# Two more experts' weight loads started in the transition, into memory of split operands and of the last blocks' sums

## The chip, the core and the metric

The kernel runs on one core of one Trainium2 chip. A core has five engines that each work through their own instructions in order: TensorE (PE in the profile; its weight loads are PEld), VectorE (DVE), ScalarE (ACT), GpSimd (POOL) and SyncE (SP, which here only issues transfers and reads registers). Sixteen DMA engines move data between the chip's memory (HBM) and the core's own memory (SBUF). The metric is the time of one execution on the device, in microseconds (us); the time given for the kernel before is the median of three runs.

## The reference

One decoder layer on a sequence of 1024 tokens with D_MODEL = 1024, all float32. Its second half is a hierarchical mixture of experts: 4 groups of 8 experts, each token takes the best group and in it the best two experts, so 2048 token-expert pairs go to 32 experts.

```
h = rms_norm(x) * (1 + sc1) + sh1                        # first half: a combined projection,
q, k, v, gu, gv, ga, gb = split(h @ w_in)                # windowed attention and a chunked gMLP,
x = x + g1 * (merged(q..gb) @ w_o)                       # merged by gates, then W_o
h = rms_norm(x) * (1 + sc2) + sh2
g_idx  = argmax(h @ w_router_g + b)                      # 1 of 4 groups
top_i  = top_k((h @ w_router_e + b)[g_idx], 2)           # 2 of its 8 experts
for each expert e, in blocks of at most 128 of its tokens xb:
    y = (silu(xb @ w_gate[e]) * (xb @ w_up[e])) @ w_down[e]   # 1024 -> 512 -> 1024
    out[tokens] += y * weight
x = x + g2 * out
return rms_norm(x, final_g)
```

The weights of one expert are three matrices of 2 MB each: gate, up and down.

## The kernel before

**Two stages.** The first, up to some 690 us, does the projections, the attention, the gMLP, W_o and the router. The second runs the 32 experts. Between them lies the transition: the router's results are counted and sorted, the tokens' rows h are stored to HBM (`h2d`), and the rows of the first experts are gathered from there.

**Order of the loads.** Every 2 MB matrix is an item of `ring2`, in the order gate0, up0, gate1, down0, up1, gate2, down1, up2, gate3, down2, up3, gate4, ...: item 7 is up2, item 8 gate3. An item goes into one of 7 buffers named `big`. `get(n)`, called where item n is used, first issues the loads up to item n+6; the SP queue issues them in order, and each waits until its buffer's last reader is through. Only the two halves of item 6 (down1) go through POOL's queue, around the first gather. Items 0 to 6 are issued before the transition ends; item 7 is the first that waits for a buffer that an expert has used.

**Units of work.** A unit is one expert or two. The first four experts stand alone, with blocks of 32, 32, 64 and 128 tokens (the units 0 to 3); after them come units of a block of 128 and one of 64 rows. A block under 128 rows multiplies float32 weights as they lie in the `big` buffer (`side`, L1504). For a block of 128 rows every matrix is split into a rounded part and the rest, in four pieces of 128x1024: ACT casts `hi` from `big` (L451) and DVE subtracts to get `lo` (L452), then 24 matmuls of three kinds follow (`mm3`, L135 to L137). There are three `hi` and three `lo` buffers, 512 KB each, in the pool `h2p`. gate3 (item 8) is the first matrix that is split; up2 (item 7) is used as it lies.

**What else stands on ACT and PE.** `x_t` transposes a block's gathered rows on PE (L1448, L1458); ACT copies the result out of PSUM as `xTh` (L1449, or L451 for a 128-row block). `a_t` does the same with the product sl of the silu (L1552, L1559 on PE; `aTh` on ACT, L1554 or L451). These copies stand on ACT in one row with the casts of the next weights. The order of the instructions on each engine is decided when the kernel is built, by a scheduler with its own idea of how long things take.

**The transition on POOL.** After the two halves of item 6 and the first two gathers, POOL issues the third gather (unit 2), works on the first two tables that list the experts' tokens (L1777, L1778; PE multiplies them at L1780), copies the gain vector into other layouts (`in_layout`, L1569, `g` from `g2r`, which PE spreads at L1826), issues the fourth gather (unit 3) and goes on with the tables. Earlier it clears the four accumulators z (L1657).

**The last blocks' sums.** For the last four experts the partial sums stay in the tiles `Z` and `YL` (2560 floats in a partition), used in the last units alone.

Of the kernel before, what the change touches and what calls it, by code (L numbers as in the profile page):

```python
# [10 lines left out]
F32 = mybir.dt.float32  # L11
F32R = mybir.dt.float32r
# [7 lines left out]
P = 128  # L20
D = 1024
# [5 lines left out]
FE = 512  # L27
# [9 lines left out]
FIRST = (0, 3, 2, 1)  # L37
# [17 lines left out]
class Ring:  # L55


    def __init__(self, bufs):
        self.bufs, self.items, self.tiles, self.issued = bufs, [], {}, 0

    def add(self, load):
        self.items.append(load)
        return len(self.items) - 1
# [4 lines left out]
            self.issued += 1  # L68

    def get(self, n):  # L70
        self.upto(n + self.bufs - 1)
        return self.tiles[n]


# [27 lines left out]
def block_kernel(ctx: ExitStack, tc: tile.TileContext, x, c, positions, rel_bias, w_ada, b_ada,  # L102
# [5 lines left out]
    w_gate, w_up, w_down = w_gate[0], w_up[0], w_down[0]  # L108
    PE, DVE, ACT, POOL, SP = nc.tensor, nc.vector, nc.scalar, nc.gpsimd, nc.sync

    def f(ap):
        return ap.bitcast(F32)
# [8 lines left out]
    def nm(s):  # L121
        uid[0] += 1
        return f"{s}_{uid[0]}"

    def bigt(shape, dt=F32):
        return big.tile([P] + shape, dt, name=nm("big"), tag="big")
# [333 lines left out]
    R = {}  # L460
# [860 lines left out]
    for i, js in ((4, w1), (5, w1), (6, w2), (7, w2)):  # L1321
        j = {4: 1, 5: 3, 6: 4, 7: 6}[i]
# [13 lines left out]
    ring2 = Ring(7)  # L1336
    jobs2 = Jobs(2)
# [19 lines left out]
    ends = flat[-4:]  # L1357
    regs = {}

    def expert_reg(c, eng):  # L1360
        if (c, eng) not in regs:
            regs[c, eng] = eng.value_load(ord_i[0:1, c:c + 1], min_val=0, max_val=NE - 1)
        return regs[c, eng]
# [5 lines left out]
    def parts_of(src):  # L1369

        return src.rearrange("(h p j) n -> p h (j n)", h=2, p=P)

    def w2_load(c, w, down, parts=1, eng=SP):
        def load():
            t = bigt([4, D] if down else [8, FE])
            th = t.rearrange("p (h j) n -> p h (j n)", h=2)
            if late:
                src = parts_of(w[8 * FIRST[c]])
                for i in range(2):
                    if late["stage"] == 0 and i == 1:  # L1380
                        gather(flat[0])
                    with tc.issue_after(R["gather" if late["stage"] or i else "h2d"].ins):
                        POOL.dma_start(th[:, i], src[:, i])
                if not late["stage"]:
                    gather(flat[1])
                late["stage"] += 1
                return t
            src = w[ds(expert_reg(c, eng), 1)].rearrange("a k n -> (a k) n") if c >= 4 else w[8 * FIRST[c]]
            src = parts_of(src)
            if parts == 1:  # L1390
                eng.dma_start(th, src)
            else:
                n = th.shape[2] * 2 // parts
                for h in range(2):
                    for k in range(0, th.shape[2], n):
                        eng.dma_start(th[:, h, k:k + n], src[:, h, k:k + n])
            return t
        return load
# [4 lines left out]
    def parts(i):  # L1403

        return P // rows_of.get(i, P)
# [19 lines left out]
    def gather(i, idx=None):  # L1425
        t = wk.tile([P, D], F32, name=nm("xg"), tag="xg")
        R["gather"] = fetch(t, h2d, IDX[i][0] if idx is None else idx, *x_rows(i))
        XG[i] = t

    Z, YL, adds = {}, {}, []  # L1430
# [134 lines left out]
    def in_layout(dst, src, q):  # L1565

        n, m = P // q, D // q
        for e in range(q):
            POOL.tensor_copy(dst[n * e:n * e + n], src[n * e:n * e + n, m * e:m * e + m])  # L1569
# [37 lines left out]
    i = 0  # L1607
# [26 lines left out]
    h2p = p2.enter_context(tc.tile_pool(name="p2hl", bufs=3, reuse_waits="tile"))  # L1634
    wk = p2.enter_context(tc.tile_pool(name="p2wk", bufs=2, reuse_waits="tile"))
# [15 lines left out]
    for i in range(2):  # L1651
        t = wk.tile([P, D], F32, name=nm("xg"), tag="xg")
        ACT.copy(t, zcol.to_broadcast([P, D]))
    for i in ends:
        Z[i] = wk.tile([P, D // parts(i)], F32, name=nm("z"), bufs=1)
        YL[i] = wk.tile([P, D // parts(i)], F32, name=nm("y"), bufs=1)
        POOL.memset(Z[i], 0.0)  # L1657
    fs = wk.tile([P, 12], F32, name="fs", bufs=1)

    ring2.upto(5)  # L1660
    late["stage"] = 0
    ring2.upto(6)
    late.clear()


    def combine_weights():
# [155 lines left out]
    def spread(dst):  # L1822

        for n in range(2):
            sl, ps = slice(512 * n, 512 * n + 512), bank()
            PE.matmul(ps, ones[0:1, :], dst[0:1, sl], start=True, stop=True)  # L1826
            ACT.copy(dst[:, sl], ps)
# [8 lines left out]
    nj = len(jobs2.jobs)  # L1836
# [49 lines left out]
    def l_put(j):  # L1886
        st_ = put(out, IDX[ends[j]][1], F["o"][j], parts(ends[j]))
        for other in F["puts"]:
            tc.declare_no_dep(st_.ins, other.ins, reason="a token's row is written once")
        F["puts"].append(st_)  # L1890

    def final():

        with tc.manual_schedule(engines={E_.DVE, E_.Activation, E_.Pool, E_.PE}):
# [27 lines left out]
            for j in (3, 0, 1, 2):  # L1922
                l_put(j)
    jobs2.hook(f_at, f_load)
    jobs2.hook(nj - 30, f_gain)
    jobs2.hook(nj - 20, lambda: (spread(F["g"]), in_layout(F[4], F["g"], 4), in_layout(F[2], F["g"], 2)))
    jobs2.hook(nj - 1, final)
# [4 lines left out]
    with tc.If(nover > 0):  # L1932
# [38 lines left out]
        with tc.For_i(0, nover, 1) as s:  # L1971
# [6 lines left out]
            for w, down in ((w_gate, False), (w_up, False), (w_down, True)):  # L1978
                t = bigt([4, D] if down else [8, FE])
# [7 lines left out]
            for z, key in ((0, "g"), (1, "u")):  # L1987
                PS[X, key] = bank()
                for kk in range(0, 8, 2):
                    wh, wl = split2(raws[z][:, kk:kk + 2])  # L1990
                    for q in range(2):
                        k = kk + q
# [14 lines left out]
        for t in range(8):  # L2007
            z, y = bigt([D]), bigt([D])
# [15 lines left out]
def build(inputs):  # L2024
    import concourse.bacc as _bacc

    nc = _bacc.Bacc("TRN2", target_bir_lowering=False, num_devices=1)
    arrays, args = {}, []
    for name in _INS:
        a = np.ascontiguousarray(inputs[name])  # L2030
        arrays[f"in_{name}_dram"] = a
        args.append(nc.dram_tensor(f"in_{name}_dram", a.shape, mybir.dt.from_np(a.dtype), kind="ExternalInput").ap())
    for i, (shape, dtype) in enumerate(_OUTS):
        dt = mybir.dt.from_np(np.dtype(dtype))
        args.append(nc.dram_tensor(f"out_{i}_dram", shape, dt, kind="ExternalOutput").ap())
    with tile.TileContext(nc) as tc:
        block_kernel(tc, *args)
    return nc, arrays
# [8 lines left out]
```

## Time and profile before

| | us |
|---|---|
| median of 3 runs (lowest, highest) | 1276.18 (1273.81, 1278.65) |
| profiled execution | 1273.97 |
| its span, first to last instruction | 1272.3 |
| PE busy in it | 1149.1 (90%) |
| DVE, ACT, POOL busy | 770.7, 554.9, 220.7 |
| mean granted TensorE clock | 0.951 of full speed |

The experts' stage takes the last 580 us or so of the span. A clock of 1.00 in a row is 2.4 GHz, 0.50 is 1.2 GHz. In rows of the timeline a bracket holds the idle time of the engine before the instruction and what ended it: "[1.62 <-ACT hi L451]" is 1.62 us of idling until ACT's instruction of line 451 had written `hi`.

### The profile page before, as it was taken

The numbers are of one execution on the slowest core, as the hardware profiler recorded it, in microseconds if no ns is written. First come the engines' busy times: TensorE is split into PE (matmuls) and PEld (weight loads), VectorE is DVE, ScalarE is ACT, GpSimd is POOL, SyncE is SP. The second block draws the span as 40 slices with busy tenths as digits, with TensorE's granted clock in tenths as the row PEclk, the third lists the DMA queues.
The fourth block names the chain that finished last, engine by engine and source line by source line (L and its number), as shares of the span: only waits on it lengthen the run. The fifth ranks groups of instructions, "written<-read, shape, count | busy, mean of one in ns | idle before, by whom it ended". The sixth has DMA issues, their size and how long they took to land. (4 is left out here: it accounts for less than half of the span.)

```text
span 1272.3 us, 18572 instructions
## 1 busy us (share of the span) xinstructions
PE 1149.1 (90%) x6873; PEld 878.3 (69%) x6874; DVE 770.7 (61%) x1685; ACT 554.9 (44%) x970; POOL 220.7 (17%) x325
## 2 busy tenths in 40 slices
PE   5999999999989999799996998998999998899961
PEld 3788887778878988688775665665665656676530
DVE  7668885567777888443498454664424635695115
ACT  4459743335525775233242344543414524674130
POOL 2600000111041000110034311121022121112201
PEclk9899999999989999899996999999999998999975
DMA  9734436547354445433956999999989999999994
GB/s 313 223 112 125 133 101 231 182 153 260 105 195 150 124 133 181 151 99 100 348 213 211 390 401 416 402 392 400 335 297 403 380 327 414 410 361 369 394 414 173
DMA packets 106345, 334.70 MB, mean 263 GB/s; under 512 B 7998, under 2 KB 52158, under 8 KB 81800
## 3 DMA queue, kind: packets, MB, share of 16 engines
q1 hardware_dynamic: 92438, 296.66, 61.4%
q0 software_dynamic: 13712, 36.77, 10.1%
q8 instruction: 55, 0.90, 0.3%
q14 instruction: 42, 0.34, 0.1%
q10 hardware_dynamic: 98, 0.03, 0.0%
HBM read 314.54 MB, written 25.71 MB: 267 GB/s over the span
## 5 line engine op out<-in xcount | busy, mean ns | idle before, releaser
L135 PE MATMUL ps<-big,hi 128*128 128x512 f32 x544 | 219.7, 404 | 11.1 <-ACT hi L451 10.8
L452 DVE TENSOR_TENSOR lo<-big,hi 128x1024 fp32r<-128x1024 f32 x156 | 185.5, 1222 | 67.5 <-ACT hi L451 66.8
L136 PE MATMUL ps<-big,hi 128*128 128x512 f32 x544 | 216.6, 398 | 4.1 <-DVE big L452 4.1
L137 PE MATMUL ps<-big,lo 128*128 128x512 f32 x544 | 215.7, 397 | 0.0
L451 ACT CAST hi<-st 128x512 fp32r<-128x512 f32 x192 | 116.2, 620 | 204.2 <-PE ps L136 115.2
L452 DVE TENSOR_TENSOR lo<-st,hi 128x512 fp32r<-128x512 f32 x192 | 135.4, 716 | 104.8 <-ACT hi L451 104.0
L451 ACT CAST hi<-big 128x1024 fp32r<-128x1024 f32 x156 | 159.4, 1050 | 69.8 <-PE ps L137 69.2
L1504 PE MATMUL ps<-big,xTh 128*32 128x128 f32 (+1 forms) x1792 | 132.2, 334 | 5.9 <-DMA big<-in_w_up_dram 3.0
L135 PEld LDWEIGHTS ps<-big,hi 128*128 128x128 f32 x544 | 104.8, 193 | 34.7 <-ACT hi L451 12.5
L136 PEld LDWEIGHTS ps<-big,hi 128*128 128x128 f32 x544 | 104.6, 192 | 28.7 <-DVE big L452 5.8
L137 PEld LDWEIGHTS ps<-big,lo 128*128 128x128 f32 x544 | 104.4, 192 | 23.1 <-DVE lo L452 1.1
L1504 PEld LDWEIGHTS ps<-big,xTh 128*32 128x32 f32 (+1 forms) x1792 | 82.8, 125 | 44.6 <-issue 12.2
L136 PE MATMUL ps<-lo,xTh 128*128 128x512 f32 x224 | 94.5, 422 | 13.1 <-DVE lo L452 13.0
L135 PE MATMUL ps<-hi,xTh 128*128 128x512 f32 x224 | 94.5, 423 | 11.2 <-ACT hi L451 11.2
L137 PE MATMUL ps<-hi,xTl 128*128 128x512 f32 x224 | 91.4, 408 | 0.0
L135 PE MATMUL ps<-hi,big 128*128 128x256 f32 (+1 forms) x256 | 88.3, 346 | 0.5 <-ACT hi L451 0.5
L136 PE MATMUL ps<-lo,big 128*128 128x256 f32 (+1 forms) x256 | 86.8, 339 | 1.1 <-DVE lo L452 1.1
L137 PE MATMUL ps<-hi,big 128*128 128x256 f32 (+1 forms) x256 | 86.4, 338 | 0.0
L1421 POOL DMA_INDIRECT zd<-y,rows_i x30 | 50.8, 1694 | 175.7 <-DVE y L1581 96.2
L1504 PE MATMUL ps<-big,aTh 128*32 128x256 f32 (+1 forms) x448 | 64.8, 511 | 12.0 <-DMA big<-in_w_down_dram 12.0
L1416 POOL DMA_INDIRECT xg<-h2d,rows_i x30 | 36.1, 1204 | 222.8 <-PE ps L1448 101.4
L1577 DVE SCALAR_TENSOR_TENSOR y<-ps,w_sb,g 128x512 f32<-128x512 f32 (+1 forms) x20 | 12.9, 643 | 89.0 <-PE ps L1504 81.8
(382 smaller groups left out, 1867.4 us busy)
## 6 DMA issues: line engine op xcount, KB each, us to landing
big<-in_w_gate_dram SPq DMA_DIRECT2D x32, 2048.0 KB
big<-in_w_up_dram SPq DMA_DIRECT2D x32, 2048.0 KB
big<-in_w_down_dram SPq DMA_DIRECT2D x30, 2048.0 KB
st<-in_w_in_dram SPq DMA_DIRECT2D x26, 1024.0 KB
st<-in_w_ada_dram SPq DMA_DIRECT2D x16, 1024.0 KB
st<-in_w_o_dram SPq DMA_DIRECT2D x10, 1024.0 KB
big<-in_x_dram SPq DMA_DIRECT2D x16, 512.0 KB
bias<-biasd POOLq DMA_DIRECT2D x16, 512.0 KB
```

What stands on the lines that cost most here:

```text
L135: PE.matmul(ps, lh, rh, start=start, stop=False)
L136: PE.matmul(ps, lh, rl, start=False, stop=False)
L137: PE.matmul(ps, ll, rh, start=False, stop=stop)
L451: ACT.copy(hi, src)
L452: return DVE.tensor_tensor(lo, src, f(hi), op=OP.subtract)
L1416: return POOL.indirect_dma_start(out=t[0:n, 0:D // q], out_offset=None, in_=in_parts(src, q), in_offset=bass.IndirectOffsetOnAxis(ap=idx[0 ...
L1421: return POOL.indirect_dma_start(out=in_parts(dst, q), out_offset=bass.IndirectOffsetOnAxis(ap=idx, axis=0), in_=t[:, 0:D // q], in_offset ...
L1504: PE.matmul(ps[n * e:n * e + n, 0:m], xt[:, s * i:s * i + n], cols_w, start=start, stop=stop)
L1577: DVE.scalar_tensor_tensor(y, ps[:, 0:D // q], w, G2p[q], op0=OP.mult, op1=OP.mult)
```

## The change

Item 7 (up2) is loaded in four pieces of 512 KB by SP, into two `hi` and two `lo` buffers that nothing has used yet. Item 8 (gate3) is loaded in four pieces by POOL, behind the second gather, into the third `hi` and `lo` buffer and into `zy0`, new memory of which the first 2048 floats are used. `Z` and `YL` become slices of a tile `zy1` that takes the same memory later: `last_sums`, 100 jobs before the end, clears it in one instruction. Since two items no longer take a `big` buffer, `get(n)` issues up to item n+8 while n is at most 7, and up to n+7 at n = 8. All other source stays; line numbers move down, by 1 up to the loads (L451 becomes L452), by 17 behind them (L1504 becomes L1521, L1569 becomes L1586), by 32 behind `last_sums` (L1777 becomes L1809).

```diff
--- before.py
+++ after.py
@@ -57,6 +57,7 @@
 
     def __init__(self, bufs):
         self.bufs, self.items, self.tiles, self.issued = bufs, [], {}, 0
+        self.apart = ()
 
     def add(self, load):
         self.items.append(load)
@@ -68,7 +69,7 @@
             self.issued += 1
 
     def get(self, n):
-        self.upto(n + self.bufs - 1)
+        self.upto(n + self.bufs - 1 + sum(i >= n for i in self.apart))
         return self.tiles[n]
 
 
@@ -1370,6 +1371,22 @@
 
         return src.rearrange("(h p j) n -> p h (j n)", h=2, p=P)
 
+    class Pieces:
+
+
+        def __init__(self, tiles):
+            self.tiles = tiles
+
+        def __getitem__(self, at):
+            k = at[1]
+            return self.tiles[k.start // 2] if isinstance(k, slice) else self.tiles[k // 2][:, k % 2]
+
+    def pieces_load(c, w, tiles, eng=SP):
+        src = parts_of(w[8 * FIRST[c]])
+        for i, t in enumerate(tiles):
+            eng.dma_start(t.rearrange("p j n -> p (j n)"), src[:, i // 2, 1024 * (i % 2):1024 * (i % 2) + 1024])
+        return Pieces(tiles)
+
     def w2_load(c, w, down, parts=1, eng=SP):
         def load():
             t = bigt([4, D] if down else [8, FE])
@@ -1651,16 +1668,31 @@
     for i in range(2):
         t = wk.tile([P, D], F32, name=nm("xg"), tag="xg")
         ACT.copy(t, zcol.to_broadcast([P, D]))
-    for i in ends:
-        Z[i] = wk.tile([P, D // parts(i)], F32, name=nm("z"), bufs=1)
-        YL[i] = wk.tile([P, D // parts(i)], F32, name=nm("y"), bufs=1)
-        POOL.memset(Z[i], 0.0)
+    def last_sums():
+        n = sum(D // parts(i) for i in ends)
+        t = wk.tile([P, 2 * n], F32, name="zy1", tag="zy", bufs=1)
+        POOL.memset(t[:, 0:n], 0.0)
+        at = 0
+        for i in ends:
+            m = D // parts(i)
+            Z[i], YL[i] = t[:, at:at + m], t[:, n + at:n + at + m]
+            at += m
     fs = wk.tile([P, 12], F32, name="fs", bufs=1)
 
     ring2.upto(5)
+    zy = wk.tile([P, 2 * sum(D // parts(i) for i in ends)], F32, name="zy0", tag="zy", bufs=1)
+    zy = zy[:, 0:2048].rearrange("p (i j n) -> p i j n", i=2, j=2)
+    hl2 = [f(h2p.tile([P, 2, FE], F32R, name=nm(t), tag=t)) for t in ("hi", "lo") * 3]
+    t7 = pieces_load(2, w_up, hl2[0:4])
+    ring2.items[7] = lambda: t7
     late["stage"] = 0
     ring2.upto(6)
     late.clear()
+    with tc.issue_after(R["gather"].ins):
+        t8 = pieces_load(3, w_gate, hl2[4:6] + [zy[:, 0], zy[:, 1]], POOL)
+    ring2.items[8] = lambda: t8
+    ring2.upto(8)
+    ring2.apart = (7, 8)
 
 
     def combine_weights():
@@ -1922,6 +1954,7 @@
             for j in (3, 0, 1, 2):
                 l_put(j)
     jobs2.hook(f_at, f_load)
+    jobs2.hook(nj - 100, last_sums)
     jobs2.hook(nj - 30, f_gain)
     jobs2.hook(nj - 20, lambda: (spread(F["g"]), in_layout(F[4], F["g"], 4), in_layout(F[2], F["g"], 2)))
     jobs2.hook(nj - 1, final)
```

**ACT, around items 14, 16 and 18.** In the kernel before, big_1235_7898 is item 14, big_1250_7973 item 16 and big_1269_8066 item 18; sl, xTh and aTh are the silu and the two copies that wait for PE:

```order
L451 CAST hi_1299_8201<-big_1235_7898 128x1024
L1537 ACTIVATE sl_1301_8223<-ps_1296_8189 128x512
L1449 COPY xTh_1310_8251<-ps_1311_8252 128x512
L451 CAST hi_1305_8234<-big_1250_7973 128x1024
L451 CAST hi_1307_8240<-big_1250_7973 128x1024
L451 CAST hi_1313_8262<-big_1250_7973 128x1024
L451 CAST hi_1316_8273<-big_1250_7973 128x1024
L451 CAST aTh_1321_8317<-ps_1320_8312 128x512
L1537 ACTIVATE sl_1328_8343<-ps_1319_8307 128x256
L451 CAST hi_1324_8327<-big_1269_8066 128x1024
L451 CAST hi_1326_8335<-big_1269_8066 128x1024
L451 CAST hi_1329_8345<-big_1269_8066 128x1024
```

In the changed kernel the same place reads, with big_1246_7972 for item 16 and big_1265_8065 for item 18 (the copy aTh in the first row is that ahead of the silu of item 14):

```order
L1571 COPY aTh_1294_8198<-ps_1293_8195 128x256
L452 CAST hi_1301_8233<-big_1246_7972 128x1024
L452 CAST hi_1303_8239<-big_1246_7972 128x1024
L1554 ACTIVATE sl_1297_8222<-ps_1292_8188 128x512
L452 CAST hi_1309_8261<-big_1246_7972 128x1024
L1466 COPY xTh_1306_8250<-ps_1307_8251 128x512
L452 CAST hi_1312_8272<-big_1246_7972 128x1024
L452 CAST hi_1320_8326<-big_1265_8065 128x1024
L452 CAST hi_1322_8334<-big_1265_8065 128x1024
L452 CAST hi_1325_8344<-big_1265_8065 128x1024
L452 CAST aTh_1317_8316<-ps_1316_8311 128x512
L1554 ACTIVATE sl_1324_8342<-ps_1315_8306 128x256
```

Before, the first cast of item 16 stands behind the copy xTh, which waits for transposes, and the first of item 18 behind the copy aTh and the silu; after, two casts of item 16 stand ahead of the silu and three ahead of xTh, and the first three of item 18 ahead of aTh and the silu. From item 10 to item 27 the casts have moved ahead in the same manner at most of the places; at item 8 it is the other way round (three casts stood ahead of the silu and xTh, and now stand behind them); from item 29 on the two orders agree.

**POOL, the end of the transition.** In the kernel before (g is the gain in other layouts, y a table, xg gathered rows):

```order
L1416 DMA xg_1172_7449<-h2d_68,tok_s_101 128x512
L1416 DMA xg_1190_7557<-h2d_68,tok_s_101 128x512
L1777 TENSOR_TENSOR y_1195_7615<-y_1195_7615,wts_77 128x2x34
L1778 TENSOR_TENSOR y_1195_7615<-y_1195_7615,pay_7458 128x2x34
L1777 TENSOR_TENSOR y_1200_7637<-y_1200_7637,wts_77 128x2x34
L1778 TENSOR_TENSOR y_1200_7637<-y_1200_7637,pay_7458 128x2x34
L1569 COPY g24_7415<-g2r_7413 32x256 x2
L1569 COPY g22_7414<-g2r_7413 64x512
L1569 COPY g24_7415<-g2r_7413 32x256 x2
L1569 COPY g22_7414<-g2r_7413 64x512
L1416 DMA xg_1217_7769<-h2d_68,tok_s_101 128x1024
```

In the changed kernel (hi, lo and zy take item 8):

```order
L1433 DMA xg_1170_7448<-h2d_68,tok_s_101 128x512
L1387 DMA hi_1166_7435<-in_w_gate_dram 128x1024
L1387 DMA lo_1167_7436<-in_w_gate_dram 128x1024
L1387 DMA zy0_7430<-in_w_gate_dram 128x1024 x2
L1586 COPY g24_7415<-g2r_7413 32x256 x4
L1586 COPY g22_7414<-g2r_7413 64x512 x2
L1433 DMA xg_1188_7560<-h2d_68,tok_s_101 128x512
L1809 TENSOR_TENSOR y_1193_7618<-y_1193_7618,wts_77 128x2x34
L1810 TENSOR_TENSOR y_1193_7618<-y_1193_7618,pay_7461 128x2x34
L1809 TENSOR_TENSOR y_1198_7640<-y_1198_7640,wts_77 128x2x34
L1810 TENSOR_TENSOR y_1198_7640<-y_1198_7640,pay_7461 128x2x34
L1433 DMA xg_1215_7781<-h2d_68,tok_s_101 128x1024
```

The four loads of item 8 stand behind the second gather; behind them the six gain copies, which before stood behind the third gather and the first two tables; the third gather and the tables now come after the copies.

**SP, behind the load of item 5** (the first row of each); each TENSOR_LOAD reads an expert's number into a register:

```order
L1391 DMA big_1169_7440<-in_w_gate_dram 128x2x2048
L1832 DMA g2r_7413<-rowd3_177 1x1024
L1362 TENSOR_LOAD ord_i_103
...
L1391 DMA big_1191_7572<-in_w_up_dram 128x2x2048
L1391 DMA big_1196_7622<-in_w_gate_dram 128x2x2048
```

In the changed kernel:

```order
L1408 DMA big_1161_7428<-in_w_gate_dram 128x2x2048
L1387 DMA hi_1162_7431<-in_w_up_dram 128x1024
L1387 DMA lo_1163_7432<-in_w_up_dram 128x1024
L1387 DMA hi_1164_7433<-in_w_up_dram 128x1024
L1387 DMA lo_1165_7434<-in_w_up_dram 128x1024
L1864 DMA g2r_7413<-rowd3_177 1x1024
L1363 TENSOR_LOAD ord_i_103
...
L1408 DMA big_1189_7575<-in_w_down_dram 128x2x2048
L1408 DMA big_1194_7625<-in_w_up_dram 128x2x2048
```

The four loads of item 7 stand ahead of the small load of `g2r`, and the register loads before the next load of weights (now item 9, down2) are ten instead of fourteen.

## Rows read from the trace of the kernel before

**Rows 1.** Waits of PE, 720 to 1028 us: us in total, times, longest.

```profile
PE ps L135 <- ACT hi L451: 12.4, 8, 2.1
PE ps L136 <- DVE lo L452: 6.2, 10, 0.8
```

**Rows 2.** Waits of PE, 1028 us to the end, the longest.

```profile
PE ps L1504 <- DMA big<-in_w_down_dram: 12.0, 6, 6.5
```

**Rows 3.** Waits of SP's DMA queue, 690 us to the end, the longest.

```profile
SPq L1391 <- PE ps L1504: 216.4, 49, 10.8
```

**Rows 4.** Windows: us, busy PE, PEld, DVE, ACT, POOL, then PEclk, DMA share, GB/s.

```profile
752.00:842.00 90.00, 80.14 (x400) 55.03 (x400) 52.58 (x62) 42.94 (x53) 15.44 (x10) 0.96 1.02 402
842.00:1028.00 186.00, 176.88 (x957) 116.74 (x955) 87.75 (x95) 68.53 (x88) 28.60 (x21) 0.98 0.95 364
1028.00:1206.00 178.00, 161.39 (x1275) 114.00 (x1274) 97.34 (x105) 78.65 (x101) 39.02 (x27) 0.97 1.00 382
```

**Rows 5.** Waits of PE, 750 to 842 us.

```profile
PE ps L135 <- ACT hi L451: 6.1, 4, 1.6
PE ps L136 <- DVE lo L452: 3.6, 5, 0.8
```

**Rows 6.** Timeline of ACT: start, us, line, operation, count, idle before.

```profile
767.36 0.58 ACT L1449 COPY xTh<-ps 128x512 f32<-128x512 f32 x1 [3.66 <-PE ps L1448]
767.84 2.94 ACT L451 CAST hi<-big 128x1024 fp32r<-128x1024 f32 x3
```

**Rows 7.** Timeline of PE around item 16.

```profile
768.94 0.51 PE L135 MATMUL ps<-hi,xTh 128*128 128x512 f32 x1 [1.62 <-ACT hi L451]
770.24 0.50 PE L136 MATMUL ps<-lo,xTh 128*128 128x512 f32 x1 [0.79 <-DVE lo L452]
...
770.81 0.55 PE L135 MATMUL ps<-hi,xTh 128*128 128x512 f32 x1
...
774.45 0.40 PE L135 MATMUL ps<-hi,xTh 128*128 128x512 f32 x1
...
777.00 0.40 PE L137 MATMUL ps<-hi,xTl 128*128 128x512 f32 x1
```

**Rows 8.** Windows of 20 us, a stretch with a lower clock.

```profile
760.00:780.00 20.00, 17.59 (x80) 11.07 (x80) 7.68 (x8) 5.65 (x7) 2.65 (x2) 0.91 1.02 403
```

**Rows 9.** Timeline of POOL in the transition.

```profile
681.95 0.53 POOL L1383 DMA_DIRECT2D big<-in_w_down_dram  x1 [1.15 <-ACT lgs L1670]
...
687.87 1.11 POOL L1416 DMA_INDIRECT xg<-h2d,tok_s  x1 [4.11 <-DVE jp L1641]
...
692.23 1.19 POOL L1416 DMA_INDIRECT xg<-h2d,tok_s  x1 [1.29 <-PE ps L1448]
695.49 0.41 POOL L1777 TENSOR_TENSOR y<-y,wts 128x68 f32<-128x68 f32 x1 [2.08 <-DVE y L932]
...
697.38 3.06 POOL L1569 COPY g<-g2r 32x256 f32<-32x256 f32 x6 [0.71 <-ACT g2r L1827]
700.71 1.06 POOL L1416 DMA_INDIRECT xg<-h2d,tok_s  x1 [0.27 <-POOL g L1569]
```

**Rows 10.** Timeline of PE from the first gather on.

```profile
690.85 1.10 PE L1448 MATMUL ps<-ident,xg 128*128 128x128 f32 x4 [4.44 <-DMA xg<-h2d,tok_s]
...
700.72 0.66 PE L1780 MATMUL ps<-y 128*128 128x68 f32 x4
```

**Rows 11.** Timeline of PE at the first split weights (item 8).

```profile
712.00 0.68 PE L1448 MATMUL ps<-ident,xg 128*128 128x128 f32 x4
...
725.21 0.50 PE L135 MATMUL ps<-hi,xTh 128*128 128x512 f32 x1
```

**Rows 12.** Windows of 4 us in the transition.

```profile
680.00:684.00 4.00, 1.44 (x9) 1.13 (x9) 3.34 (x25) 2.11 (x3) 2.35 (x6) 0.50 0.71 214
684.00:688.00 4.00, 1.13 (x14) 0.94 (x13) 3.43 (x26) 0.00 (x0) 0.13 (x1) 0.50 0.58 227
...
696.00:700.00 4.00, 4.00 (x68) 2.56 (x70) 0.64 (x3) 2.97 (x5) 3.02 (x9) 1.00 0.03 6
```

## The prediction

> **What bounds the kernel now.** I first asked whether the engines wait for weights at all, since the change brings weights earlier. The waits of PE from 720 to 1028 us are 12.4 us for ACT's `hi` and 6.2 us for DVE's `lo`, and no transfer is among them [rows 1]. Transfers are waited for only later; the largest such sum behind 1028 us is 12.0 us for down matrices [rows 2], near the end. The other side agrees: SP's loads wait for buffers that PE still reads, 216.4 us in 49 waits [rows 3]. So in the first half of the expert stage the reader should see a DMA that is full (share 1.02 from 752 to 842 us, 0.95 from 842 to 1028) and yet not what PE waits for, because it runs ahead of PE by as much as the seven buffers allow. PE is the bound there: busy for 80.14 of 90 us and 176.88 of 186 us [rows 4].
>
> Then I asked why PE loses time at all from 752 to 842 us. Its waits there are 6.1 us for `hi` and 3.6 us for `lo`, 9.7 us in nine waits [rows 5], which is all but 0.2 us of the 9.86 us that PE is idle [rows 4]. One shows the cause. At 767.36 ACT copies xTh after idling for 3.66 us, for the transposes of PE; only then come the casts of item 16, at 767.84 [rows 6]. The weights could have been cast in that idling, had they not stood behind the copy. PE, done with its transposes, idles for 1.62 us until the first cast and 0.79 us until the first `lo` [rows 7]. Such a wait has a second price: at 770.81 matmuls slow down until 774.45, nine of them in 3.64 us, where eleven take 2.55 us afterwards (774.45 to 777.00, 0.232 us each) [rows 7]; the granted clock of that window is 0.91 [rows 8], so a part of it ran at 1.2 GHz. That costs 3.64 - 9 x 0.232 = 1.55 us. One more such stretch lies from 808 to 812 us (the mean from 752 to 842 us is 0.96 [rows 4]).
>
> What is gained before 1028 us should last to the end. From 1028 to 1206 us the DMA share is 1.00 at 382 GB/s [rows 4], that is, a stream without slack that starts when PE frees a buffer; if PE frees it earlier, the stream begins and ends earlier.
>
> **The change part by part.** *The loads by themselves: 0.* Items 7 and 8 arrive earlier and so do the items behind them, as far as buffers allow. PE waits for none of these [rows 1], so nothing is bought by that alone.
>
> *The order of ACT's casts: -9.7 and -3.1 us.* What the change does to PE comes by way of the order. In the rows of order, two casts of item 16 now stand ahead of the silu and a third ahead of xTh, and three of item 18 ahead of aTh. So the first cast is done while ACT would have idled, and PE finds `hi` and `lo` ready. The orders differ up to item 27, which is the stretch of rows 5; I take all nine waits as gone, 9.7 us, and both slow stretches, 2 x 1.55 = 3.1 us. The bounds: nothing, if the waits come back at other copies, and 12.8 us. I take the upper end since the stalled casts need only data that is there; with three `hi` buffers a cast can run no more than three pieces ahead, which is enough for the first.
>
> *POOL in the transition: +2.1 us.* The gain copies start at 697.38, when ACT has spread the gains, and end by 700.44; the tables t0 and t1 were done before that, from 695.49 on [rows 9]. Now the copies come first, then the third gather (1.19 us to issue), then t0 (0.41 and 0.29 us): 700.44 + 0.3 + 1.19 + 0.7 + small gaps, about 702.8. PE wants t0 at 700.72 [rows 10] and waits for 2.1 us; behind it stand the matmuls of unit 1, in PE's own order. Bounds: 0, if the copies find their input earlier, and 3.06 + 1.19 = 4.3 us. The four issues of item 8 on POOL cost about 0.53 us each [rows 9], 2.1 us in all; they end near 693.5 and lie in the wait for the gains. The cover gone, they would add up to 2.1 us.
>
> *A slow stretch behind that wait: +1.6 us.* A wait of PE of 2.1 us is like the pair of 1.62 and 0.79 in rows 7, behind which the clock fell. I count one, at the price above.
>
> *The third gather:* issued at 692.23 before [rows 9], now near 700.7. Its rows are wanted at 712.00 [rows 11], later still with the waits above: 11 us. The first gather, issued at 687.87, was there at 690.85 [rows 9, 10], 3 us. With a DMA at full load it will take longer; I count 0.
>
> *DMA in the transition: +1.0 us.* PE idles for 4.44 us for the first gather, until 690.85 [rows 10], so this transfer is on the path. Item 7 adds 2 MB, 5.2 us at the 402 GB/s of rows 4. Up to 688 us the DMA has (1 - 0.71) x 4 + (1 - 0.58) x 4 = 2.8 us of room [rows 12], so 2.4 us of it could still be under way when the gather starts. The bounds are 0 (the gather's own issue waits for DVE at 687.87 [rows 9]) and 2.4 us. The queues share, so I take 1.0. Item 8 is issued behind the second gather and finds room (share 0.03 from 696 to 700 us [rows 12]).
>
> By the Trainium skill ("DMA: Bandwidth & Descriptors", section "Issuing engines are not separate DMA queues") transfers of all issuing engines run on the same 16 DMA engines and interleave, so POOL's own queue would shield no gather. No row of the kernel before shows it for this gather; by this rule the term would be nearer its upper bound of 2.4, the sum -6.3 us and the median 1269.9.
>
> *Item 8's casts: +0.4 us.* The first cast writes into a buffer that holds up2 until its matmuls are through, and stands behind xTh. PE wants it at 725.21 [rows 11]; the last of up2's matmuls end just there, but the first buffer is free some 2.7 us before, enough for one cast (2.94 / 3 = 0.98 us [rows 6]) and a `lo`. Bounds 0 and 2.4 us (the two waits of rows 7); near the lower one.
>
> *Clearing the sums.* One instruction near the fourth unit in place of four in the transition: POOL is busy for under a fifth of that stretch (15.44 of 90 us [rows 4]). Nothing.
>
> The sum: -9.7 - 3.1 + 2.1 + 1.6 + 1.0 + 0.4 = -7.7 us. The profiled execution, 1273.97, lies 2.2 us under the median of 1276.18; it would be 1266.3, the median 1268.5.
>
> **Rivals.** *A: no change.* PE and not the order is what lasts: the waits leave one copy and come back at the next, or the schedule's idea of the times is off. For it: nine waits remain behind 842 us with the order unchanged (18.6 in rows 1 less 9.7). Against: data and buffers allow the earlier casts. If half of the 12.8 us is regained, 12.8 / 2 - 5.1 = 1.3 us are left: 1274.9.
>
> *B: the loads count.* The stream is the bound and 4 MB less to load behind 700 us ends 4.19 MB / 402 GB/s = 10.4 us earlier, less the 3.5 us of waits for tables, gather and casts: 1269.3 with the order of no account; with both, 1263. For it: the share of 1.02 [rows 4]. Against: no wait for a transfer [rows 1].
>
> *C: slower.* Gather 1 waits behind item 7: with the two queues in turns, all of item 7 (5.2 us) ahead of it and the tables' 4.3 us on top, with two slow stretches (3.1 us), 12.6 us are lost against at most 6.4 regained: 1282.4. It decides if the gather lands 5 us later than at 690.85. Against: item 7 is issued near 670 us, 18 us before the gather.
>
> **How the numbers follow.** The forecast's chance is 0.55, with its own range from 1264 to 1273 (no slow stretch and no late gather, or a third of the waits kept). A 0.23, B 0.12, C 0.10. The range of 8 in 10 leaves out half of C and the tails of A and B: 1262 to 1279. A measurement of this kernel tells 0.5% from no change, 6.4 us: faster is under 1269.8, slower over 1282.6. The forecast lies 1.3 us under the first bound, 0.34 of its 0.55 are faster; with all of B and a little of A 0.49. Slower is half of C and a tail: 0.09. The rest, 0.42, is within.
>
> **What would show it.** Waits of PE for `hi` and `lo` between 750 and 842 us should fall from 9.7 us to under 3, and the window of 20 us with a clock of 0.91 at item 16 should be 1.00. A wait for POOL's first table should stand at about 701 us, near 2 us, and PE's first gather should end its wait at 691 to 693. The stream behind item 60 should start some 8 us before 1028. The prediction is wrong if the waits for `hi` move to other items, if the first gather is late by more than 3 us, or if a gather or a load is what PE waits for between 700 and 850 us.

## The result, and the profile after

The changed kernel takes 1263.12 us (median; 1260.36 to 1268.21) against 1277.2 us before, measured side by side: a ratio of 0.9901, 95% interval 0.988 to 0.9922. By the ratio that is 12.6 us faster (0.0099 x 1277.2; the medians lie 14.1 apart); 7.7 were forecast. The profiled execution shown here is the slowest of its four (1268.21, span 1266.5 us), which matters below.

First the windows that answer to [rows 4] (us; busy PE, PEld, DVE, ACT, POOL; then clock, DMA share, GB/s):

```profile
752.00:842.00 90.00, 90.00 (x483) 64.26 (x483) 61.45 (x71) 50.16 (x61) 18.52 (x12) 1.00 1.02 403
842.00:1028.00 186.00, 176.87 (x1008) 116.33 (x1006) 82.52 (x89) 63.96 (x85) 30.53 (x23) 0.97 0.95 360
```

From 752 to 842 us PE is busy for all of the 90.00 us (80.14 before), and the clock is 1.00 (0.96 before). The DMA share is 1.02 as before. Behind 842 us PE is busy for as long as before, 176.87 us against 176.88, though the window holds somewhat later work, as PE is ahead.

The waits of PE from 720 to 1028 us, as in [rows 1]:

```profile
PE ps L136 <- ACT hi L452: 6.3, 4, 2.1
PE ps L137 <- DVE lo L453: 2.6, 5, 0.8
```

Of 18.6 us 8.9 are left, all behind 842 us, where the order of the instructions is the old one. For a hi or a lo between 720 and 842 us PE waits no more at all (in the second profile of the changed kernel, below, one wait of 0.63 us is left, at 838 us).

ACT's timeline where item 16 is cast, and PE's behind it ([rows 6, 7] of before):

```profile
765.29 1.05 ACT L452 CAST hi<-big 128x1024 fp32r<-128x1024 f32 x1 [0.30 <-PE ps L138]
766.72 1.05 ACT L452 CAST hi<-big 128x1024 fp32r<-128x1024 f32 x1 [0.38 <-PE ps L138]
768.07 0.60 ACT L1554 ACTIVATE sl<-ps 128x512 f32<-128x512 f32 x1 [0.30 <-PE ps L138]
768.57 1.04 ACT L452 CAST hi<-big 128x1024 fp32r<-128x1024 f32 x1
772.33 0.59 ACT L1466 COPY xTh<-ps 128x512 f32<-128x512 f32 x1 [2.73 <-PE ps L1465]
```

```profile
771.55 0.75 PE L1465 MATMUL ps<-ident,xg 128*128 128x128 f32 x4
772.05 0.47 PE L136 MATMUL ps<-hi,xTh 128*128 128x512 f32 x1
```

Two casts stand ahead of the silu (768.07) and a third (768.57) ahead of the copy xTh (772.33). When PE is done with its transposes at 772.05, `hi` and `lo` are there: there is no idling, and the next 17 matmuls start 0.22 to 0.31 us apart, without a slow stretch.

Item 27 shows what this sums up to. It begins at 841.08 before, and at 832.43 after, though PE's transposes ahead of unit 2 began at 712.00 before [rows 11] and at 717.81 after (below). The way from there to item 27 took 129.08 us and takes 114.62: 14.5 us less. The experiments come back to this way, since it leaves out the transition and the first stage, whose length varies.

```profile
841.08 0.74 PE L135 MATMUL ps<-hi,aTh 128*128 128x512 f32 x2 [1.41 <-ACT hi L451]
```

```profile
832.43 0.73 PE L136 MATMUL ps<-hi,aTh 128*128 128x512 f32 x2
```

The transition, PE first:

```profile
692.40 1.10 PE L1465 MATMUL ps<-ident,xg 128*128 128x128 f32 x4 [7.03 <-DMA xg<-h2d,tok_s]
...
706.29 0.70 PE L1812 MATMUL ps<-y 128*128 128x68 f32 x4
...
717.81 0.67 PE L1465 MATMUL ps<-ident,xg 128*128 128x128 f32 x4
```

The first gather comes 1.55 us later than in [rows 10], and the way from it to 717.81 has become 4.3 us longer (25.4 against 21.15 us), without a wait at PE's first table (706.29); the two waits on the way are 0.72 and 0.98 us in both, so it lies in a clock that stayed at 1.2 GHz for longer. Whether that belongs to the change is a question for the experiments. POOL does what the rows of order say:

```profile
693.84 1.07 POOL L1387 DMA_DIRECT2D zy<-in_w_gate_dram  x2
699.70 0.83 POOL L1586 COPY g<-g2r 32x256 f32<-32x256 f32 x2 [4.79 <-ACT g2r L1859]
703.85 1.06 POOL L1433 DMA_INDIRECT xg<-h2d,tok_s  x1 [0.28 <-POOL g L1586]
704.98 0.30 POOL L1809 TENSOR_TENSOR y<-y,wts 128x68 f32<-128x68 f32 x1
```

The last thing to read is SP's load behind item 60: 1028.17 before, 1020.92 after, 7.25 us earlier.

```profile
1028.17 0.37 SPq L1391 DMA_DIRECT2D big<-in_w_up_dram  x1
```

```profile
1020.92 0.37 SPq L1408 DMA_DIRECT2D big<-in_w_up_dram  x1
```

### The profile page after: what moved, and what is told of

It reads as the page before. It is cut to its first block, busy times and chain, and to the rows that moved or that the text cites. A ratio compares the mean times of both kernels' runs of the same rounds, so it can differ in the third digit from the quotient of the medians.

```text
span 1266.5 us, 18598 instructions
## 1 busy us (share of the span) xinstructions
PE 1150.1 (91%) x6874; PEld 878.3 (69%) x6874; DVE 771.9 (61%) x1685; ACT 555.9 (44%) x970; POOL 222.8 (18%) x326
## 5 line engine op out<-in xcount | busy, mean ns | idle before, releaser
L453 DVE TENSOR_TENSOR lo<-big,hi 128x1024 fp32r<-128x1024 f32 x152 | 181.6, 1222 | 72.3 <-ACT hi L452 71.7
L452 ACT CAST hi<-st 128x512 fp32r<-128x512 f32 x192 | 116.2, 620 | 208.6 <-PE ps L137 126.7
L452 ACT CAST hi<-big 128x1024 fp32r<-128x1024 f32 x152 | 156.2, 1050 | 72.1 <-PE ps L138 71.3
L1521 PE MATMUL ps<-big,xTh 128*32 128x128 f32 (+1 forms) x1760 | 131.5, 339 | 6.3 <-DMA big<-in_w_up_dram 3.0
L1521 PEld LDWEIGHTS ps<-big,xTh 128*32 128x32 f32 (+1 forms) x1760 | 82.5, 127 | 45.5 <-issue 13.1
L1521 PE MATMUL ps<-big,aTh 128*32 128x256 f32 (+1 forms) x448 | 64.8, 511 | 11.6 <-DMA big<-in_w_down_dram 11.6
L812 POOL TENSOR_TENSOR sg<-sg,sg 128x512 f32<-128x512 f32 x16 | 23.6, 1479 | 213.7 <-DVE sg L811 184.9
```

The costliest lines, as they stand in the source:

```text
L452: ACT.copy(hi, src)
L453: return DVE.tensor_tensor(lo, src, f(hi), op=OP.subtract)
L812: p_ = POOL.tensor_tensor(ga, ga, gb, op=OP.add)
L1521: PE.matmul(ps[n * e:n * e + n, 0:m], xt[:, s * i:s * i + n], cols_w, start=start, stop=stop)
```

## The experiments

Theory 1: the order of the casts, subtractions and transposes is the gain; the loads themselves buy nothing and cost the transition something. Theory 2: the weights' earlier arrival is the gain. Each run below has its own runs of the kernel before beside it (1273.3 to 1274.8 us).

**The changed kernel again.** No edit.

> The changed kernel once more, as the measure for the others. Both theories: about 1.0% below the kernel before (1263 against 1277 us), with no wait of PE for hi or lo from 720 to 842 us. Whether the stretch at 1.2 GHz behind the first gather ends near 705 us, as in its first profile, or earlier, is open: near 696 to 700 if the first profile was an unlucky one; the span should be shorter by half of the difference.

1261.17 us, ratio 0.9908 (0.9879 to 0.9937). So the change is worth 0.9 to 1.0%, and the first profile was a long one: this one has a span of 1259.6 us.

**ACT's order alone.** Edges that only fix the order on an engine, and make nothing wait for a result, are laid between the instructions of a list; the list is ACT's order in the changed kernel, from the third cast of item 10 to the last of item 25, and the kernel is the one before.

```diff
+def act_order(tc):
+    for (a, i), (b, j) in zip(ORDER, ORDER[1:]):
+        tc.add_manual_dep(LOG[b][j].ins, LOG[a][i].ins.name,
...
     jobs2.run()
+    act_order(tc)
```

> The kernel before with its own loads, but with the order of ACT's casts and copies from item 10 to item 29 forced to be that of the changed kernel. Theory 1, the order of the casts is the gain: the nine waits for hi and lo between 750 and 842 us go from 9.7 us to under 2 (a few could stay where the data lands late, at items 12 and 14), and with the two slow stretches the time falls by 10 to 13 us, to about 1265, as there is no cost in the transition. Theory 2, the earlier loads are the gain: the casts now wait for the data, nothing or little is gained, 1274 to 1278.

1267.47 us, 0.9953 (0.993 to 0.9976): half of the gain.

**The old order of ACT with the early loads** is the mirror of it, with the same edit in the changed kernel and ACT's old order in the list.

> The changed kernel with its early loads, but with the order of ACT's casts and copies from item 10 to item 29 forced to be that of the kernel before. Theory 1: the waits of 9.7 us come back and the costs of the transition stay, so 1277 to 1281, no faster than before. Theory 2: most of the gain stays, 1264 to 1268.

1268.32 us, 0.9963 (0.9942 to 0.9984): the other half. By these two runs neither theory holds. But the lists held ACT alone; the scheduler was free to place PE's transposes and DVE's subtractions, and in the second run it placed some of PE's as in the changed kernel. The waits of PE from 720 to 842 us with ACT's order alone (the lines of the source have moved by 13):

```profile
PE ps L149 <- DVE lo L465: 3.9, 5, 1.2
PE ps L148 <- ACT hi L464: 1.4, 1, 1.4
PE ps L150 <- DVE xTl L465: 1.0, 1, 1.0
```

ACT is cured, but for one cast, that of item 27 (at 837.20 us), to which the list does not reach; and DVE is late: 3.9 us for `lo`, 1.0 for xTl (the small part of a block's rows, which DVE subtracts as it does `lo`). So the runs had cut the order in two, not parted it from the loads. **All three orders, old loads**, and the reverse:

```diff
+def in_order(tc, nc):
+    at = {i.name: i for i in nc.cur_bb.bb.instructions}
+    for names in ORDER:                  # PE, ACT, DVE
+        for a, b in zip(names, names[1:]):
+            tc.add_manual_dep(at["I-%d" % b], "I-%d" % a,
...
     jobs2.run()
+    in_order(tc, nc)
```

> The kernel before with its own loads, but with the orders of PE, ACT and DVE from item 10 on forced to be those of the changed kernel (the run with ACT's order alone left PE's transposes and DVE's subtractions where the scheduler put them, and gained 8.8 us between items 4 and 36 against 13.1). If the orders are the whole gain: 13 us between items 4 and 36, no wait for hi or lo from 720 to 842 us, and a time of 1260 to 1264, since the weights of the kernel before land 10 us and more ahead of their use. If the early loads have a part of their own: waits for hi from item 10 to 16, where the data lands latest, and a gain of 8 to 10 us.

1265.28 us, 0.9922 (0.9893 to 0.9951). Nothing of the loads is changed in it, and PE's waits from 720 to 842 us and its busy time are nearly those of the changed kernel:

```profile
PE ps L1563 <- DVE sl L1553: 0.3, 1, 0.3
```

```profile
752.00:842.00 90.00, 89.70 (x475) 63.65 (x473) 60.88 (x71) 48.02 (x58) 16.69 (x11) 1.00 1.02 404
```

PE's way from the transposes of unit 2 to item 27 is 834.54 - 719.32 = 115.22 us, against 114.62 in the changed kernel:

```profile
719.32 0.67 PE L1459 MATMUL ps<-ident,xg 128*128 128x128 f32 x4
...
834.54 0.73 PE L146 MATMUL ps<-hi,aTh 128*128 128x512 f32 x2
```

By its time alone the run would not decide: 9.9 us of gain (0.0078 x 1274.8) lie in the range that I had given for a part of the loads, 8 to 10 us, and 1265.28 lies above the 1260 to 1264 given for the orders. By the waits and by this way it does.

> The changed kernel with its early loads, but with the orders of PE, ACT and DVE from item 10 on forced to be those of the kernel before. If the orders are the whole gain: the nine waits return (9.7 us between 750 and 842 us), nothing is gained between items 4 and 36, and the time is 1274 to 1279. If early data helps by itself: some of the waits stay away, a gain of 5 us or more there.

1277.74 us, 1.0021 (0.9998 to 1.0044): with the early loads and the old orders nothing is gained. The waits are back, eight of them up to 842 us and the ninth, of item 27, at 848.19:

```profile
PE ps L147 <- ACT hi L463: 4.7, 3, 1.6
PE ps L148 <- DVE lo L464: 3.6, 5, 0.8
```

```profile
719.10 0.67 PE L1476 MATMUL ps<-ident,xg 128*128 128x128 f32 x4
...
848.19 0.73 PE L147 MATMUL ps<-hi,aTh 128*128 128x512 f32 x2 [1.41 <-ACT hi L463]
```

The way from unit 2 to item 27 is 129.09 us, and 129.08 in the kernel before. This settles it for that stretch: of 14.5 us the orders give 13.9 with the old loads, and the loads give nothing with the old orders. So what the change did for PE was done when the kernel was built: the scheduler put the casts ahead of the copies. That it did so because it took the weights to be there earlier is the likely reason, but no run shows it.

**Item 7 late.**

```diff
-    t7 = pieces_load(2, w_up, hl2[0:4])
...
     with tc.issue_after(R["gather"].ins):
+        t7 = pieces_load(2, w_up, hl2[0:4], POOL)
         t8 = pieces_load(3, w_gate, hl2[4:6] + [zy[:, 0], zy[:, 1]], POOL)
```

> The changed kernel with item 7 loaded by POOL behind the second gather, in front of item 8, in place of SP near 670 us. If item 7's transfer is what makes the last store of h late (688.5 in place of 683.8 us), and this makes DVE wait for 1.9 us and the first gather come 1.55 us later, then DVE's wait for the store goes, PE's wait for the first gather ends at about 690.9 in place of 692.4, and the time is 1 to 2 us under that of the changed kernel. If it is something else, PE's first transposes stay at 692.4. Item 7 is wanted at 727 us and should still be there in time.

1264.75 us, 0.9936 (0.9916 to 0.9957): not the 1 to 2 us less that were expected, and not measurably different from the changed kernel (0.9908 in its second comparison), since the intervals overlap. The wait itself did what was expected. In the first profile of the changed kernel DVE waited for the store of h:

```profile
688.63 0.19 DVE L1729 TENSOR_REDUCE ol<-ol 128x4 f32<-128x32 f32 x1 [1.94 <-DMA h2d<-h]
```

With item 7 late this wait is gone. PE waited for the first gather for 7.0 us in that profile, 6.2 us in the second profile of the same kernel, and 4.4 us with item 7 late. The cause of the late gather is shown, then, and that it is worth some 2 us on PE; that the whole kernel is faster without it is not.

The 4.4 us look like the 4.44 of [rows 10], but the transition is shorter than that of the kernel before. From DVE's last MAX8 of the router (682.15, 682.14 and 682.79 us) to PE's first transposes it took 8.70 us before, 10.26 in the first profile of the changed kernel (9.47 in the second), and 7.63 with item 7 late:

```profile
690.42 1.10 PE L1465 MATMUL ps<-ident,xg 128*128 128x128 f32 x4 [4.39 <-DMA xg<-h2d,tok_s]
```

So the early item 7 costs 1.8 to 2.6 us here, and something else in the change gives 1.1 us back. By the traces it is the clearing of the sums. In the kernel before, POOL's four clears stand in the transition, and two small instructions of DVE beside them take 1.24 and 1.12 us; in the changed kernel the clears have gone to 735 us, and the same two take 0.15 and 0.22:

```profile
682.47 1.30 POOL L1657 MEMSET z<- 128x512 f32 x4
```

```profile
682.56 1.24 DVE L913 CAST si<-sf 128x2 int32<-128x2 f32 x1
682.67 1.12 DVE L893 TENSOR_TENSOR oh<-iota_u,ei 128x64 f32<-128x64 uint32 x1
```

```profile
682.54 0.15 DVE L914 CAST si<-sf 128x2 int32<-128x2 f32 x1
682.66 0.22 DVE L894 TENSOR_TENSOR oh<-iota_u,ei 128x64 f32<-128x64 uint32 x1
```

All four profiled kernels with the clears there show it (1.0 to 1.5 us), and none of the ten without. No run moves the clears alone.

**PE kept busy in its idle time.**

```diff
+    warm = bank((4, P))
+    with tc.issue_after(R["tab_mm"].ins):
+        for _ in range(18):
+            w_ = PE.matmul(warm, ones_b, ones_b.unsqueeze(1).to_broadcast([P, 4, P]), start=True, stop=True)
+    with tc.issue_after(w_.ins):
+        x_t(flat[0])
```

> The changed kernel with 18 matmuls of 128x512 in bf16, of which nothing is used, on PE between the transition's last small matmuls and the first transposes, where PE idles for 7 us. If the long stretch at 1.2 GHz behind the first gather (to 705 us in one profile of the changed kernel) comes from PE's idling, the clock is at 1.00 when the transposes start or soon after, the stretch from item 0 to item 4 is 3 to 6 us shorter than in that profile, and the time is 2 to 4 us under the changed kernel. If the clock doesn't follow PE's idling there, no difference.

1268.93 us, 0.9951 (0.9927 to 0.9976): not faster than the changed kernel but rather slower. The clock follows: in the profile the first transposes take 0.72 us in place of 1.10.

```profile
683.71 6.31 PE L1855 MATMUL ps<-ones_b 128*128 128x512 bf16 x18
689.94 0.72 PE L1465 MATMUL ps<-ident,xg 128*128 128x128 f32 x4
...
700.25 0.66 PE L1812 MATMUL ps<-y 128*128 128x68 f32 x4 [2.28 <-POOL y L1810]
```

With PE that much faster, the wait that I had forecast is there: 2.28 us for POOL's first table, at 700.25. In the changed kernel PE was late by more than that and found the table ready. The slow stretch that I had forecast behind this wait is there as well:

```profile
702.00:704.00 2.00, 2.00 (x22) 1.40 (x22) 0.60 (x2) 0.07 (x1) 1.07 (x4) 0.50 1.01 417
704.00:706.00 2.00, 2.00 (x22) 1.55 (x21) 0.56 (x2) 0.00 (x0) 0.46 (x2) 0.66 1.04 427
```

By these two rows it costs about 2 x 0.50 + 2 x 0.34 = 1.7 us, an estimate; so the early clock's gain is spent again. The profiled execution (span 1259.4 us) is as short as the changed kernel's. The longer ones (up to 1274.5 us) had a lower mean clock, 0.939 to 0.946 against 0.951 to 0.956 in the three shortest; why stays open.

**The order as a rule.** For each copy and silu on ACT I counted how many casts stand ahead of it beyond the pieces that PE has used up when it makes the copy's input. With three hi buffers three are possible. For the 15 copies and silus from the last cast of item 8 to the last of item 20, in ACT's order:

```
before  3 3 3 1 3 0 0 3 1 0 0 0 3 0 3
after   3 3 3 3 3 3 3 3 3 3 3 3 3 3 3
```

Wherever PE waited before, the count was under three at a copy or silu shortly ahead. The reverse does not hold: the next silu, at 799.0 us in the changed kernel, has a count of one, and PE waits for nothing there. From item 27 on both kernels have such places, and the waits of [rows 1] that are left. So the rule was forced on the rest, by a list for ACT in the changed kernel (`in_order` as above).

> The changed kernel with ACT's order from item 29 on forced by a rule read off its own first part: every copy out of PSUM and every silu stands behind as many casts as the three hi buffers allow, three more than PE has used up by then. If the waits are made by the order, the waits for hi between 842 and 1028 us fall from 6.3 us to under 2 and the ones behind 1028 too, PE reaches item 60 some 8 to 12 us earlier, and the time falls by 5 to 10 us, unless the weights then land too late (their landing is 12 to 15 us ahead of their use at the tightest items). If the waits have another cause, they stay.

1273.52 us, 0.9986 (0.9964 to 1.0008): all gain lost, with one wait of 17.0 us for a copy xTh.

I took PE's moved transposes for the reason, and **kept PE's order** by a second list:

> The rule of the last run once more, now with PE's own order kept as in the changed kernel, so that no copy stands behind more than the three casts that can run before PE is through (in the last run one copy stood behind seven, and PE waited 17.0 us for it). If the order makes the waits: no wait for hi between 842 and 1028 us (6.3 us in the changed kernel, 2.6 us for lo), PE 10 to 12 us earlier at item 60, and, as the stream of weights behind it starts with PE, 8 to 11 us less than the changed kernel, about 1251. If the gain stops at what the weights allow, PE waits for transfers at items 47 to 50, whose weights land 12 us ahead of their use in the changed kernel.

1273.28 us, 0.9992 (0.9974 to 1.001). That reason was wrong, the wait stays: 16.86 us at 926 us. ACT's timeline tells why:

```profile
939.49 2.94 ACT L463 CAST hi<-big 128x1024 fp32r<-128x1024 f32 x3 [24.64 <-DMA big<-in_w_gate_dram]
942.34 0.58 ACT L1477 COPY xTh<-ps 128x512 f32<-128x512 f32 x1
```

```profile
942.96 1.97 PE L1532 MATMUL ps<-big,xTh 128*64 128x256 f32 x8 [16.86 <-ACT xTh L1477]
```

Between items 40 and 46 the weights are used unsplit (three units of one block of 64 rows each follow one another there), so the next casts are those of item 47. The rule put three of them ahead of a copy; they waited 24.64 us for the weights' transfer, the copy behind them, and PE for the copy. It is the same fault the other way round.

> The same order, with item 7 loaded by POOL behind the second gather. If the early item 7 costs the transition 1 to 1.5 us (from the landing of item 0 to its first matmul: 81.9 us in the kernel before and in the runs without an early item 7, 82.1 to 82.7 with it), this is 1 us under the run above; a measurement of five rounds may not tell that.

1274.76 us, 1.0002 (0.9985 to 1.0018): the same wait (20.5 us), nothing to be told apart.

> The kernel before with its own loads, and the three orders of the run above. If the early loads are of no use at all, this is as fast as the run above or 1 to 3 us faster, since the transition costs less. If they are the room into which a faster PE moves, PE runs into weights that have not landed: they land only 1.4 to 3.5 us ahead of their use at items 27 to 35 in the run with the orders alone, against 12 us in the changed kernel; then most of the gain behind 842 us is lost, and the time is 1258 to 1263.

1281.53 us, 1.0045 (1.0025 to 1.0066), with a wait of 19.0 us at that place. The question of this run, whether the early loads are room for a faster PE, is answered with yes by the distance to the run with the same orders and the early loads: 1.0045 against 0.9992, though the same wait weighs on both. The traces show it ahead of that place. ACT's casts wait for transfers five times from 815 to 930 us, 26.8 us in all; with the early loads they wait for none there.

```profile
ACT hi L462 <- DMA big<-in_w_down_dram: 12.0, 2, 7.0
ACT hi L462 <- DMA big<-in_w_gate_dram: 7.8, 2, 4.8
ACT hi L462 <- DMA big<-in_w_up_dram: 7.0, 1, 7.0
```

PE's way from item 27 to item 33 is 37.77 us in this run, 32.27 in the other. So the early loads, worth nothing to the orders of the changed kernel, are worth 5.5 us to a tighter one.

Last, **the rule up to item 39**, ahead of the unsplit items:

> The changed kernel with the rule applied to the copies from item 27 to item 39 alone. In the two runs before it, the rule also put copies of blocks that use their weights unsplit (items 40 to 46) behind casts of item 47, whose weights land only 12 us ahead of their use, and PE waited 17 us for such a copy near 926 us; up to there PE had gained 7.7 us over the changed kernel. If the order is the cause of the waits and the held copy the cause of that loss: no wait above 2 us between 842 and 1028 us, PE 7 to 9 us earlier than in the changed kernel from item 36 on, and the time 5 to 9 us under it, 1252 to 1257. If the gain is lost again further on, the time is that of the changed kernel, 1261.

1256.53 us, 0.9877 (0.9857 to 0.9898), the fastest here; against the changed kernel (0.9901 and 0.9908) the intervals still overlap. PE's longest wait from 842 to 1028 us is 1.6 us, and its way from item 27 to item 39 is 77.63 us, against 86.87 in the first profile of the changed kernel; the time lies in the range expected. Its window:

```profile
842.00:1028.00 186.00, 179.17 (x1094) 116.96 (x1096) 84.27 (x92) 67.11 (x89) 36.82 (x24) 1.00 0.99 375
```

PE is busy for 179.17 us from 842 to 1028 us (176.87), at a clock of 1.00 (0.97), and 6.8 us of idling are left there. The DMA share has risen to 0.99 (0.95), so there is little room for weights to come sooner.

## Why the prediction was right

**That PE doesn't wait for weights, so loads alone bring nothing**: right, shown by the early loads with the old orders (1.0021, and 129.09 us to item 27).

**The order, -9.7 and -3.1 us**: the mechanism was right and the size near. All nine waits went, both slow stretches went, and the way to item 27 is 14.5 us shorter, 1.7 more than the 12.8 forecast; what the 1.7 us are is not resolved. I had put it down to ACT's casts alone; ACT's order alone gives 0.47 of the 0.78% that all three orders give, and the rest comes by DVE's subtractions and PE's transposes that moved with them.

**The transition, +5.1 us**: too much, and a large part of why 12.6 was measured where 7.7 was forecast. The late first gather was 1.55 us in one profile (1.0 forecast), but that is luck, for it is the balance of two terms. Item 7's transfer costs 1.8 to 2.6 us (1.0 forecast), and moving the clears, which I had put at nothing, gives 1.1 us back.

By the Trainium skill ("DMA: Bandwidth & Descriptors", section "Issuing engines are not separate DMA queues") transfers started by different engines run on the same 16 DMA engines and interleave. The trace agrees: with item 7's load issued early by SP, the last store of h on POOL's queue is late, DVE waits 1.94 us for it, and this wait goes when item 7 is loaded later. That DVE stands between the store and the gather I had not seen.

The wait for POOL's table, +2.1 us, is hidden, for PE runs at 1.2 GHz there and comes later than the table; it showed at 2.28 us when PE was made faster, and the slow stretch behind it, +1.6, showed with it. In the changed kernel both stay away behind the table. In its second profile, though, a stretch at a clock of 0.57 lies just ahead of the table (696 to 700 us), so these two terms depend on where the clock returns, and are not settled. Item 8's casts, +0.4, cost no wait at PE. So by the rows 1.55 us of the 5.1 are seen, and the rest lies within what the clock does there by itself.

**That the gain lasts to the end**: right for the most part. In the first profile PE is 8.65 us ahead at item 27, SP's load behind item 60 is 7.25 us earlier, and the span ends 5.8 us earlier. In the second profile the three are 15.0, 13.8 and 12.7 us. So 2.3 to 2.9 us are lost behind item 27, for a reason that stays open. From 14.5 less 1.55 and less these, 10.0 to 10.6 us are left; 12.6 and 11.7 were measured (0.9901 and 0.9908), and their intervals reach down to 10.0 and 8.0.

The rivals: A fell, for the waits went away and did not move. B fell by the run with the old orders. C did not come, the gather was late by 1.55 and not by 5 us.

## What to carry to other kernels

An early load can change the order that a scheduler builds, and that may be the whole gain: compare the two orders before explaining a gain by data, and part the two by forcing all engines' orders, not one. On an engine that works in order, work that needs only buffers (casts of the next weights) belongs as far ahead of work that waits for another engine as the buffers allow, but never ahead by data that has not landed: casts ahead of copies gain 14.5 us here, and casts of weights still under way cost 17 us at one place. Earlier loads are then worth as much as the tighter order needs them. The cost of a wait in a place with a low clock or an idle engine is not its price in the row; ask what else is late there.

## What the runs showed of the hardware

The stretch at 1.2 GHz in the transition ends at very different times in code that is the same there. In the kernel before the clock is back to 2.4 GHz (1.00) from 696 us on, 5 us behind PE's first transposes at 690.85; in the run with the orders alone, whose transition is that of the kernel before, only from 708 us, 14 us behind them (694.22). The windows of the kernel before, and of that run:

```profile
694.00:696.00 2.00, 2.00 (x29) 1.39 (x22) 2.00 (x11) 0.00 (x0) 0.51 (x2) 0.55 0.43 129
696.00:698.00 2.00, 2.00 (x20) 0.76 (x18) 0.64 (x3) 0.99 (x2) 1.23 (x5) 1.00 0.00 0
```

```profile
704.00:706.00 2.00, 2.00 (x31) 1.56 (x33) 0.00 (x0) 1.22 (x3) 1.31 (x3) 0.50 0.63 131
...
708.00:710.00 2.00, 2.00 (x33) 1.62 (x33) 0.85 (x3) 0.27 (x1) 0.48 (x2) 1.00 1.01 428
```

PE idled for 4.4 us ahead of the first transposes in both. In the first profile of the changed kernel it was late too: 0.50 up to 706 us, 14 us behind the transposes at 692.40, with 7.03 us of idling ahead of them. The way from the first gather's transposes to those of unit 2 is 21.15 us in the kernel before and 24.5 to 25.1 us in the three runs with its loads, 25.41 and 22.81 us in the two profiles of the changed kernel. A single profile is thus off by some 4 us at this place alone, which is more than most terms of the sum; and no cost or gain of the change can be read from it there.

While POOL cleared four tiles of 128x512, a CAST of 128x2 on DVE took 1.24 us in place of 0.15, and ended as the clears did (683.80 and 683.77 us). These clears held up DVE on the critical path; the second small instruction behind them was drawn out as well (1.12 us in place of 0.22).
